# A decoder trunk step: gMLP's layer norm in two VectorE passes, other chain distances, another tile order

## The chip, the cores and the metric

The kernel runs on one core of a Trainium2 chip. A core has five engines that work side by side and wait for each other by semaphores: TensorE (PE in the profile; its weight loads are PEld) multiplies matrices, VectorE (DVE) and ScalarE (ACT) do elementwise work and can read PE's results in PSUM, GpSimd (POOL) does elementwise work in SBUF alone, SyncE (SP) here only issues transfers. The metric is the time on the device for one execution, in microseconds (us), as the median of several runs.

## The reference

One layer of a decoder, for 1024 prompt tokens and 64 sample tokens with the same weights. In short:

```python
x = layer_norm(ALPHA * x + 0.5 * swiglu(x, f1...), ln1_g, ln1_b)
z = x @ w_in + b_in
u, v, q, k, vm, o, ig, fg = split(z)
u, v = gelu(u), gelu(v)                                  # 4 gMLP heads of 128 columns
vn = layer_norm(v, gm_ln_g, gm_ln_b)                     # over a head's 128 columns
gm = u * (tril(W_s) @ vn + b_s)                          # inside chunks of 128 tokens
h_ml = sigmoid(o) * mlstm(silu(conv(q)), silu(conv(k)), vm, ig, fg)   # 4 mLSTM heads
mix = concat(head_rms(gm, gm_out_g), head_rms(h_ml, ml_out_g))
x = layer_norm(ALPHA * x + mix @ w_out, ln2_g, ln2_b)
x = layer_norm(ALPHA * x + 0.5 * swiglu(x, f2...), ln3_g, ln3_b)
```

The layer norm of the change is the one that makes `vn`: mean and variance over the 128 columns of a head, (v - mean) times 1/sqrt(var + eps), times a gain, plus a bias.

## The kernel before

The tokens stand in nine tiles: tiles 0 to 7 are 128 prompt tokens each, tile 8 is the 64 sample tokens. All matrix products are made in a split form: an operand is cut in a high and a low part (a copy on ACT, a subtraction on DVE, L237 and L238 for activations, L122 and L124 for weights), and the product is the sum of two or three products of parts.

The program goes through these stages: the first FFN (`Up`, `Down`), layer norm 1 with the transposes that follow it, the input projection with the gMLP and mLSTM work between its matmuls, the output projection with layer norm 2, the second FFN, layer norm 3.

**The input projection** runs token tile by token tile. `zunit` (L948 on) computes one tile: 24 matmuls for a prompt tile, 16 for the sample tile, whose token parts stand side by side so that one product fewer is needed; its two halves of the result are added when it is evicted (`add_psum`, L984 and L986, the second only for tile 8). Loops over all nine tiles are made for: `vm` (two times, columns of the mLSTM values), `gmlp_units(h)` (four times, u and v of a gMLP head) and the second half of `o`. Between them `heads(h)` makes q and k of an mLSTM head. The order is heads 0 and 1, units 0, heads 2, units 1, heads 3, `o`, units 2, units 3.

**Weights.** `Weights` keeps blocks of weights in six buffers; a set for one loop is four blocks, so up to two blocks of the next set can stand ready. In the last tile of a loop (`release`), a block is given back after each pair of its columns has been used, and the next block of the plan is then loaded, copied (L122) and subtracted (L124). The subtraction is on POOL for every second block of the input projection, otherwise on DVE.

**Background chains.** What isn't a large matmul is written as Python generators. `bg.tick()` lets each active chain run up to its next `yield`. `zunit` ticks after every `tick_every` matmuls and once at its end: with 6, four ticks in a prompt tile and three in the sample tile. `bg.until(...)` ticks, without matmuls between, until the chains named have ended. So the number of `yield`s in a chain is a distance, in ticks, between its steps. The order of ticks is the order in which instructions are written; the framework then sets each engine's queue by priority in that order and by its own estimate of when operands are ready, so the queues in the trace are not exactly in program order. All waits are put in by the framework.

**A gMLP chain** (`gmlp`, L1371 on) belongs to a head and three tiles: group (h, 0) is tiles 0 to 2, (h, 1) tiles 3 to 5, (h, 2) tiles 6 to 8. It is spawned when the third of its tiles has been evicted and has gone through GELU (L1448) into a buffer `ge`. Its steps: statistics on DVE (L1384, L1385); 1/sqrt by a power on POOL (`rsqrt`, L242 and L243); 4 yields; the normalisation on DVE (L1391); gain and bias on POOL (L1397), a multiply and an add over all three tiles; 8 yields; the product with the chunk's matrix (`pmix`, L1406); 2 yields; times u (L1412) and sums of squares on ACT (L1415); 2 yields; a second 1/sqrt on POOL; 4 yields; the last scaling into the mixer tile `y` on DVE (L1425; `y` is `ya` for tiles 0 to 3 and `yb` for the others). There are three `ge` buffers: a unit that opens a new group waits by `bg.until` for the chain that was spawned three groups earlier.

**mLSTM chains** (`mlstm(h)`) wait for the convolution of k, then three yields, then go through the chunks. Their last scaling is L1367.

**The output projection** goes over tiles 0 to 3, then 8, 4 to 7, in four column groups each. Ahead of it, a barrier `bg.until` waits for the mLSTM chains and for groups (3, 0) and (3, 1). `mix_xt(t)` transposes the mixer tile t (L251), splits it (L237, L238) and loads the residual; the first three are started at once, each later one three tiles ahead.

Of the kernel before, what the change touches and what calls it, by code (L numbers as in the profile page):

```python
# [29 lines left out]
KSC = float(P) ** -0.5  # L30
BIG = 1.0e30
WO_GROUPS = ((0, 1, 2, 3), (8, 4, 5, 6, 7))
WCOL = 528
YW = 1040
OU, OV, OQ, OK, OVM, OO, OG = 0, 512, 1024, 1536, 2048, 2560, 3072
# [67 lines left out]
class Weights:  # L103
# [10 lines left out]
    def _issue(self):  # L114
        nc = self.nc
        i = self.issued
        key = self.plan[i]
        n = 528 if key == ("o", 0, key[2]) else 512
        raw = self.pool.tile([P, WCOL], F32, tag="r", name=f"wr{i}", bufs=4)
        nc.sync.dma_start(raw[:, :n], self.src[i][:, :n])  # L120
        wt = self.pool.tile([P, 2, WCOL], F32R, tag="u", name=f"w{i}")
        nc.scalar.copy(wt[:, 0, :n], raw[:, :n])  # L122
        eng = nc.gpsimd if not key[0].startswith("wo") and i % 2 else nc.vector
        eng.tensor_sub(wt[:, 1, :n], raw[:, :n], wt[:, 0, :n].bitcast(F32))  # L124
        self.tiles[key] = wt
        self.issued += 1
# [57 lines left out]
def trunk_kernel(ctx: ExitStack, tc: tile.TileContext, a):  # L184
# [964 lines left out]

    for c in range(2):  # L1150
        wts = token_weights("vm", c)
        for t in range(NT):
            rows = _rows(t)

            def evict(p, t=t, rows=rows, c=c):
                ye = y[:rows, t, c * 260:(c + 1) * 260].rearrange("p (h e) -> p h e", h=2)
                add_psum(t, ye[:, :, 0:P], p[:, 0:256].rearrange("p (h e) -> p h e", h=2),
                         bc1[:rows, 512 + c * 256:512 + (c + 1) * 256].rearrange("p (h e) -> p h e", h=2))
                G.memset(ye[:, :, P:P + 1], 1.0)
                G.memset(ye[:, :, P + 1:P + 2], 0.0)  # L1160

            zunit(t, wts, 256, evict, "pv", release=t == 8)


    cvt = spare[:, 0:216].rearrange("p (b j) -> p b j", b=8)
# [47 lines left out]
    def mlstm(h):  # L1213
        while ("conv", "k", h) not in bg.finished:
            yield
        for _ in range(3):
            yield
        q, k = conv_out[("q", h)], conv_out[("k", h)]
        p1s, wts_, kws, p2s, cns = {}, {}, {}, {}, {}
# [151 lines left out]
    def gmlp(h, ts, ge, wsr, wss):  # L1371
# [12 lines left out]
            V.bn_stats(st[:rows], ge[:rows, j, 0:P])  # L1384
            V.bn_aggr(mv[:rows, j, :], st[:rows])  # L1385
        rsqrt(rs[:, 0:3], mv[:, :, 1], EPS, 3)
        for _ in range(4):
            yield
        for j, t in enumerate(ts):
            rows = _rows(t)  # L1390
            V.tensor_scalar(ge[:rows, j, 0:P], ge[:rows, j, 0:P], mv[:rows, j, 0:1], rs[:rows, j:j + 1],  # L1391
                            op0=ALU.subtract, op1=ALU.mult)
        parts = [(P, slice(0, 2)), (TS, slice(2, 3))] if tail else [(P, slice(0, 3))]
        for op, c0 in ((ALU.mult, 0), (ALU.add, 512)):
            for rows, js in parts:
                v = ge[:rows, js, 0:P]
                G.tensor_tensor(v, v, bc4[:rows, c0 + h * P:c0 + (h + 1) * P].unsqueeze(1).to_broadcast(list(v.shape)), op=op)  # L1397
        for _ in range(8):
            yield
        if tail:  # L1400
            nc.sync.dma_start(a["gvp"][:, hs], ge[:, 1, 0:P])
# [14 lines left out]
        yield  # L1416
        yield
        rsqrt(rs[:, 3:6], rs[:, 3:6], EPS, 3, scale=1.0 / P)
        for _ in range(4):
            yield  # L1420
        while ("m", h) not in bg.finished:
            yield
# [5 lines left out]
    def gmlp_units(h):  # L1428
        wts = token_weights("vu", h)
        bvu = bc3[:, h * 256:(h + 1) * 256]  # L1430
        wsr = m2.tile([P, P], F32, tag="wsr", name="wsr")
        wss = m2.tile([TS, TS], F32, tag="wss", name="wss")
        nc.sync.dma_start(wsr, a["wsT"][:, h * P:(h + 1) * P])
        nc.sync.dma_start(wss, a["wsS"][:, h * TS:(h + 1) * TS])
        G.tensor_tensor(wsr, wsr, tri, op=ALU.mult)
        G.tensor_tensor(wss, wss, tri_s, op=ALU.mult)
        for t in range(NT):
            rows = _rows(t)
            if t % 3 == 0:
                ge_no = 3 * h + t // 3  # L1440
                if ge_no >= 3:
                    bg.until(("gm",) + divmod(ge_no - 3, 3))
                ge = m2.tile([P, 3, 256], F32, tag="ge", name="ge", bufs=3)

            def evict(p, t=t, rows=rows, ge=ge):
                gt = ge[:rows, t % 3, :]
                add_psum(t, gt, p[:, 0:256], bvu[:rows])
                S.activation(gt, gt, AF.Gelu_apprx_tanh)  # L1448
                if t % 3 == 2:
                    bg.spawn(("gm", h, t // 3), gmlp(h, [t - 2, t - 1, t], ge, wsr, wss))  # L1450

            zunit(t, wts, 256, evict, "pgm", tick_every=6, release=t == 8)

    def heads(h):
        wt = [W.get(("qk", h, kp)) for kp in range(4)]
# [23 lines left out]


    wts = token_weights("o", 1)
    for t in range(NT):
        rows = _rows(t)

        def evict(p, t=t, rows=rows):
# [4 lines left out]
            bg.until(("epa", 2))  # L1490
            V.scalar_tensor_tensor(hml(rows, t, 2), og[:rows, 0:P], 1.0, hml(rows, t, 2), op0=ALU.add, op1=ALU.mult)

        zunit(t, wts, 256, evict, "po", tick_every=6, release=t == 8)
    bg.finished.add(("o", 1))
    nc.sync.dma_start(a["cv"], cvt)
    gmlp_units(2)
    gmlp_units(3)

    bg.newest_first = False
    bg.until(*[("epb", h) for h in range(H)], ("gm", 3, 0), ("gm", 3, 1), *[("m", h) for h in range(H)])  # L1500


    def mix_xt(t):
        rows = _rows(t)
        while t >= 6 and ("gm", 3, 2) not in bg.finished:
            yield
        put_xt(t, 0, transposes(t, [j * 130 for j in range(4)]))
        yield
        put_xt(t, 1, transposes(t, [520 + j * P for j in range(4)]))
        nc.sync.dma_start(y[:rows, t, 0:D], x1d[t * P:t * P + rows, :])  # L1510
        yield
# [243 lines left out]
```

## Time and profile before

| | us |
|---|---|
| median of 3 runs | 1951.69 (1951.45 to 1952.05) |
| profiled execution | 1949.92 |
| its span | 1948.1 |

The profile shows one execution. The span goes from its first to its last instruction. Busy times are sums per engine; a row of a group gives busy time and mean length of one instruction, then, behind a bar, how long the engine sat idle just ahead of such instructions and what ended that. A row of an order of time gives start, length, engine, line, operation, `output<-inputs`, the shape and a count; idle time ahead of it stands in square brackets with the instruction that ended it. Matmuls are pipelined: two that follow each other overlap in the rows, so a row's length over its count is not exactly the pace. Some matmul records can be missing.

The stages lie about so: first FFN up to 723 us, input projection from there to 1107 us, output projection to about 1230 us, second FFN to the end.

### The profile page before, as it was taken

What the parts mean: (1) busy time and instruction counts of PE and PEld (TensorE: products, weight loads), DVE (VectorE), ACT (ScalarE), POOL (GpSimd) and SP (SyncE); (2) the same over time, 40 slices, a digit from 0 to 9 for tenths busy, and PEclk for the clock granted to TensorE, in tenths of its full rate; (3) what the DMA queues carried; (4) which work ended last, traced back from release to release, by engine and by line L of the source; (5) the groups of instructions that cost most, each with busy time, mean ns of one, the idle gap of its engine ahead of it and who ended that gap; (6) DMA issues with size and microseconds to landing.
All of it is one profiled execution on the core that took longest, in us unless ns stands there. A gap on an engine that the chain in (4) does not pass through costs nothing.

```text
span 1948.1 us, 27285 instructions
## 1 busy us (share of the span) xinstructions
PE 1920.8 (99%) x10207; PEld 1628.4 (84%) x10207; DVE 1315.1 (68%) x2313; ACT 770.6 (40%) x1507; POOL 474.2 (24%) x404
## 2 busy tenths in 40 slices
PE   8999999999999999999999899999999999999997
PEld 7888888888788889988889899888888888888885
DVE  8876555656856585367876866986665665685657
ACT  5544444444222242164453333554444444422222
POOL 0222222222433031114423400012222222243302
PEclk9999999999999999999999999999999999999999
DMA  6444443336876533111211263244444333687643
GB/s 217 154 149 158 140 149 138 130 123 222 316 261 223 182 126 106 44 45 50 63 36 47 79 227 105 87 155 148 149 149 155 134 134 123 216 321 260 225 159 116
DMA packets 100892, 293.15 MB, mean 150 GB/s; under 512 B 19224, under 2 KB 26392, under 8 KB 97944
## 3 DMA queue, kind: packets, MB, share of 16 engines
q1 hardware_dynamic: 80600, 218.01, 34.1%
q10 hardware_dynamic: 20160, 73.41, 9.5%
q8 instruction: 80, 1.31, 0.3%
q14 instruction: 52, 0.43, 0.1%
HBM read 197.77 MB, written 93.60 MB: 150 GB/s over the span
## 4 chain that ended last, share of the span: by engine, by line
PE 55%; DVE 5%; POOL 1%; ACT 1%; issue 1%; DMA 0%; DVEq 0%; ACTq 0%; POOLq 0%
PE px L381 12%; PE pw L381 6%; PE pd L750 6%; PE pw L750 5%; PE pq L973 5%; PE pw L957 4%; PE pz L381 3%; PE pgm L957 3%; PE pv L957 3%; PE po L957 2%; PE psm L397 2%; PE psm L759 1%; PE tp L251 1%; DVE yb L306 1%; DVE yb L303 0%
## 5 line engine op out<-in xcount | busy, mean ns | idle before, releaser
L381 PE MATMUL px<-xo,uop 128*128 128x512 f32 x2112 | 504.5, 394 | 6.1 <-ACT uop L372 6.1
L381 PEld LDWEIGHTS px<-xo,uop 128*128 128x128 f32 x2112 | 392.9, 189 | 91.1 <-ACT uop L372 6.3
L373 DVE TENSOR_TENSOR uop<-ur,uop 128x512 fp32r<-128x512 f32 x264 | 193.4, 748 | 112.5 <-ACT uop L372 112.2
L381 PE MATMUL pw<-xo,uop 128*128 128x512 f32 x1056 | 250.0, 392 | 0.0
L381 PEld LDWEIGHTS pw<-xo,uop 128*128 128x128 f32 x1056 | 198.1, 188 | 44.3
L750 PE MATMUL pd<-wop,hop 128*128 128x512 f32 x960 | 227.7, 394 | 0.3 <-DVE rsq L242 0.2
L750 PEld LDWEIGHTS pd<-wop,hop 128*128 128x128 f32 x960 | 179.8, 188 | 42.8 <-DVE yb L721 0.6
L372 ACT CAST uop<-ur 128x512 fp32r<-128x512 f32 x264 | 158.5, 620 | 109.4 <-PE psm L397 69.1
L750 PE MATMUL pw<-wop,hop 128*128 128x512 f32 x792 | 188.5, 394 | 0.2 <-DVE yb L721 0.2
L237 ACT CAST wop<-wd 128x512 fp32r<-128x512 f32 x132 | 80.0, 620 | 248.0 <-DVE ya L721 123.9
L750 PEld LDWEIGHTS pw<-wop,hop 128*128 128x128 f32 x792 | 148.0, 188 | 35.8 <-DVE yb L721 1.0
L362 POOL TENSOR_TENSOR s<-ur,ur 128x1024 f32<-128x1024 f32 x18 | 43.8, 2432 | 512.6 <-DMA hd<-hw 260.9
L238 DVE TENSOR_TENSOR hw<-c,hw 128x512 fp32r<-128x512 f32 x120 | 96.6, 805 | 71.3 <-ACT hw L237 70.4
L381 PE MATMUL pz<-xo,uop 128*128 128x512 f32 x528 | 127.7, 397 | 0.0
L238 DVE TENSOR_TENSOR wop<-wd,wop 128x512 fp32r<-128x512 f32 x132 | 108.4, 832 | 27.2 <-ACT wop L237 26.7
L381 PEld LDWEIGHTS pz<-xo,uop 128*128 128x128 f32 x528 | 97.5, 188 | 22.3
L237 ACT CAST hw<-c 128x512 fp32r<-128x512 f32 x120 | 74.3, 619 | 75.9 <-DVE c L503 45.7
L957 PE MATMUL pgm<-w,xt 128*128 128x256 f32 x768 | 101.5, 288 | 1.1 <-DVE w L124 0.6
L397 PEld LDWEIGHTS psm<-uop,xs 128*128 128x128 f32 x704 | 95.3, 189 | 7.8 <-ACT uop L372 0.3
L957 PEld LDWEIGHTS pgm<-w,xt 128*128 128x128 f32 x768 | 94.7, 191 | 5.3 <-issue 3.4
L397 PE MATMUL psm<-uop,xs 128*128 128x256 f32 x704 | 98.0, 281 | 0.0
L957 PE MATMUL pw<-w,xt 128*128 128x256 f32 x768 | 97.4, 284 | 0.5 <-ACT xt L237 0.5
(341 smaller groups left out, 2849.8 us busy)
## 6 DMA issues: line engine op xcount, KB each, us to landing
hd<-hw ACTq DMA_DIRECT2D x140, 512.0 KB, 3.1
hop<-hd SPq DMA_DIRECT2D x132, 512.0 KB, 4.7
ur<-in_wu SPq DMA_DIRECT2D x94, 512.0 KB, 3.8
wd<-in_wd SPq DMA_DIRECT2D x22, 1024.0 KB, 7.3
wr<-in_ws SPq DMA_DIRECT2D x76, 256.0 KB, 2.9
hopx<-hd SPq DMA_DIRECT2D x8, 512.0 KB, 6.0
hsd<-sm SPq DMA_DIRECT2D x20, 192.0 KB, 1.9
hs<-hsd SPq DMA_DIRECT2D x18, 192.0 KB, 6.5
```

What stands on the lines that cost most here:

```text
L237: S.copy(hi, src)
L238: V.tensor_sub(dst[ix + (1,)], src, hi.bitcast(F32))
L251: TE.transpose(pv[:, j, :rows], y[:rows, t, c0:c0 + P], ident[:rows, :rows])
L306: V.scalar_tensor_tensor(yt, yt, mv[:rows, 2:3], b_t[:rows], op0=ALU.mult, op1=ALU.add)
L362: eng.tensor_tensor(s1, a21, a22, op=ALU.add)
L372: S.copy(op[:, 0], sj)
L373: V.tensor_sub(op[:, 1], sj, op[:, 0].bitcast(F32))
L381: TE.matmul(ps, lhsT=units[k // 2][:, wi, c0:c0 + P], rhs=self.xo[m][:, k, xi, :], start=start and k == 0 and j == 0, stop=k == 3 and j == ...
L397: TE.matmul(ps, lhsT=self.xs[:, which, k, :], rhs=units[k // 2][:, wi, (k % 2) * 256:(k % 2 + 1) * 256], start=first and k == 0 and wi == ...
L750: TE.matmul(p, lhsT=hop[:, hi, i * P:(i + 1) * P], rhs=wop[:, wi, :], start=start and pi == 0 and j == 0, stop=pi == len(pairs) - 1 and j ...
L957: TE.matmul(p[:, :n], lhsT=xl(t, k, xi), rhs=wk[:, wi, kk * n:(kk + 1) * n], start=(i == 0), stop=(i == last - 1))
L973: TE.matmul(p, lhsT=wt[k // 2][:, wi, c0:c0 + P], rhs=st["xt"][(c, k // 4)][:, k % 4, xi, :], start=(i == 0), stop=(i == 23))
```

## The change

1. Of the weight blocks, the odd ones among the first eight are subtracted on DVE instead of POOL.
2. Loops over all nine tiles, in `vm`, the second `o` and `gmlp_units`, take the order 0 to 5, 8, 6, 7. A group of the gMLP is spawned behind tiles 2, 5 and 7.
3. `mlstm` has five yields instead of three ahead of its first chunk.
4. The layer norm of `gmlp` is made in two DVE passes: (v - mean) times gain, which doesn't need the 1/sqrt and is issued right behind it; then times 1/sqrt, plus bias. POOL's two affine steps are gone. The yields are 5, 5, 2, 2, 7 in place of 4, 8, 2, 2, 4.
5. The barrier ahead of the output projection waits for group (3, 0) alone; `mix_xt(t)` waits for the group of its own tile.

```diff
+TOKS = (0, 1, 2, 3, 4, 5, 8, 6, 7)
...
-        eng = nc.gpsimd if not key[0].startswith("wo") and i % 2 else nc.vector
+        eng = nc.gpsimd if not key[0].startswith("wo") and i % 2 and i >= 8 else nc.vector
...
-        for t in range(NT):
+        for t in TOKS:
...
-            zunit(t, wts, 256, evict, "pv", release=t == 8)
+            zunit(t, wts, 256, evict, "pv", release=t == TOKS[-1])
...
-        for _ in range(3):
+        for _ in range(5):
             yield
         q, k = conv_out[("q", h)], conv_out[("k", h)]
...
         rsqrt(rs[:, 0:3], mv[:, :, 1], EPS, 3)
-        for _ in range(4):
-            yield
         for j, t in enumerate(ts):
             rows = _rows(t)
-            V.tensor_scalar(ge[:rows, j, 0:P], ge[:rows, j, 0:P], mv[:rows, j, 0:1], rs[:rows, j:j + 1],
-                            op0=ALU.subtract, op1=ALU.mult)
-        parts = [(P, slice(0, 2)), (TS, slice(2, 3))] if tail else [(P, slice(0, 3))]
-        for op, c0 in ((ALU.mult, 0), (ALU.add, 512)):
-            for rows, js in parts:
-                v = ge[:rows, js, 0:P]
-                G.tensor_tensor(v, v, bc4[:rows, c0 + h * P:c0 + (h + 1) * P].unsqueeze(1).to_broadcast(list(v.shape)), op=op)
-        for _ in range(8):
+            v = ge[:rows, j, 0:P]
+            V.scalar_tensor_tensor(v, v, mv[:rows, j, 0:1], bc4[:rows, h * P:(h + 1) * P], op0=ALU.subtract, op1=ALU.mult)
+        for _ in range(5):
+            yield
+        for j, t in enumerate(ts):
+            rows = _rows(t)
+            v = ge[:rows, j, 0:P]
+            V.scalar_tensor_tensor(v, v, rs[:rows, j:j + 1], bc4[:rows, 512 + h * P:512 + (h + 1) * P],
+                                   op0=ALU.mult, op1=ALU.add)
+        for _ in range(5):
             yield
...
         rsqrt(rs[:, 3:6], rs[:, 3:6], EPS, 3, scale=1.0 / P)
-        for _ in range(4):
+        for _ in range(7):
             yield
...
-        for t in range(NT):
+        for t in TOKS:
             rows = _rows(t)
-            if t % 3 == 0:
+            if t in (0, 3, 8):
...
-                if t % 3 == 2:
-                    bg.spawn(("gm", h, t // 3), gmlp(h, [t - 2, t - 1, t], ge, wsr, wss))
+                if t in (2, 5, 7):
+                    t0 = t // 3 * 3
+                    bg.spawn(("gm", h, t // 3), gmlp(h, [t0, t0 + 1, t0 + 2], ge, wsr, wss))
...
-    bg.until(*[("epb", h) for h in range(H)], ("gm", 3, 0), ("gm", 3, 1), *[("m", h) for h in range(H)])
+    bg.until(*[("epb", h) for h in range(H)], ("gm", 3, 0), *[("m", h) for h in range(H)])
...
-        while t >= 6 and ("gm", 3, 2) not in bg.finished:
+        while ("gm", 3, t // 3) not in bg.finished:
             yield
```

More of the change, by code (lines that the diff above doesn't have):

```diff
@@ L1448, in evict @@
                 S.activation(gt, gt, AF.Gelu_apprx_tanh)
-                if t % 3 == 2:
-                    bg.spawn(("gm", h, t // 3), gmlp(h, [t - 2, t - 1, t], ge, wsr, wss))
-            zunit(t, wts, 256, evict, "pgm", tick_every=6, release=t == 8)
+                if t in (2, 5, 7):
+                    t0 = t // 3 * 3
+                    bg.spawn(("gm", h, t // 3), gmlp(h, [t0, t0 + 1, t0 + 2], ge, wsr, wss))
+            zunit(t, wts, 256, evict, "pgm", tick_every=6, release=t == TOKS[-1])
     def heads(h):
@@ L1481, in trunk_kernel @@
     wts = token_weights("o", 1)
-    for t in range(NT):
+    for t in TOKS:
         rows = _rows(t)
@@ L1491, in evict @@
             V.scalar_tensor_tensor(hml(rows, t, 2), og[:rows, 0:P], 1.0, hml(rows, t, 2), op0=ALU.add, op1=ALU.mult)
-        zunit(t, wts, 256, evict, "po", tick_every=6, release=t == 8)
+        zunit(t, wts, 256, evict, "po", tick_every=6, release=t == TOKS[-1])
     bg.finished.add(("o", 1))
```

## The prediction

> **What bounds the kernel now.** I read the page first: the engines' shares, the slices, the chain of work that ended last.
>
> ```profile
> span 1948.1 us, 27285 instructions
> PE 1920.8 (99%) x10207; PEld 1628.4 (84%) x10207; DVE 1315.1 (68%) x2313; ACT 770.6 (40%) x1507; POOL 474.2 (24%) x404
> ...
> PE 55%; DVE 5%; POOL 1%; ACT 1%; issue 1%; DMA 0%; DVEq 0%; ACTq 0%; POOLq 0%
> ```
>
> PE is the bound: 1948.1 - 1920.8 = 27.3 us of the span are idle on it, and the change removes no matmul. So the most it can give is idle PE time, and time in which PE is busy but slow. Where that lies, the busy times by stretch tell (columns: stretch, length, then busy us and number of instructions of PE, PEld, DVE, ACT and POOL, granted clock, DMA share, GB/s):
>
> ```profile
> 0.00:20.00 20.00, 14.15 (x54) 11.01 (x55) 13.28 (x22) 14.52 (x24) 0.39 (x7) 1.00 0.90 328
> ...
> 700.00:740.00 40.00, 38.97 (x247) 34.37 (x247) 37.74 (x74) 21.10 (x38) 14.60 (x41) 1.00 0.53 171
> ...
> 850.00:900.00 50.00, 50.00 (x368) 45.62 (x367) 38.61 (x100) 32.25 (x78) 16.68 (x25) 1.00 0.11 24
> ...
> 1050.00:1100.00 50.00, 47.10 (x360) 44.30 (x359) 39.20 (x108) 13.74 (x55) 21.98 (x35) 0.97 0.11 35
> 1100.00:1130.00 30.00, 26.59 (x212) 24.56 (x211) 24.06 (x58) 14.68 (x40) 9.70 (x17) 1.00 0.47 153
> ...
> 1930.00:1948.00 18.00, 6.54 (x28) 4.67 (x26) 13.94 (x26) 2.49 (x4) 5.09 (x4) 0.77 0.29 117
> ```
>
> The first and the last stretch hold 5.9 and 11.5 us of the idle time, and the change touches neither. What it can reach is 2.9 us in 1050:1100, 3.4 us in 1100:1130 and about 1 us in 700:740. The third column from the right, the clock, is 0.97 in 1050:1100: there is more there than the idle time. Cut finer:
>
> ```profile
> 1070.00:1075.00 5.00, 5.00 (x44) 5.00 (x44) 2.55 (x11) 1.41 (x7) 1.96 (x5) 1.00 0.26 107
> 1075.00:1080.00 5.00, 2.17 (x13) 1.58 (x12) 4.49 (x10) 1.86 (x5) 2.17 (x3) 0.96 0.00 0
> 1080.00:1085.00 5.00, 4.93 (x30) 4.63 (x30) 4.17 (x12) 2.36 (x9) 2.78 (x5) 0.70 0.66 186
> 1085.00:1090.00 5.00, 5.00 (x43) 4.80 (x42) 4.37 (x12) 0.83 (x2) 2.94 (x5) 1.00 0.15 47
> ...
> 1106.00:1118.00 12.00, 8.59 (x62) 7.05 (x61) 10.89 (x26) 6.82 (x19) 4.41 (x8) 1.00 0.44 140
> 1118.00:1130.00 12.00, 12.00 (x101) 11.51 (x100) 8.47 (x22) 5.97 (x15) 1.05 (x2) 1.00 0.73 243
> ```
>
> Count matmuls: 1075:1085 ran 13 + 30 = 43 in 10 us, as many as 1085:1090 ran in 5. **Hole one** so costs 5.0 us: 2.9 us idle, about (1 - 0.96) x 5 + (1 - 0.70) x 5 = 1.7 us of lowered clock behind it, the rest short waits. 1106:1118 ran 62 where the next 12 us ran 101, so at that rate it lost 12 x (1 - 62/101) = 4.6 us: **hole two**. Both lie in gMLP's last head and the start of the output projection. PE's order of time shows what ended each gap:
>
> ```profile
> 1073.94 1.59 PE L957 MATMUL pgm<-w,xt 128*128 128x256 f32 x12
> 1077.30 0.94 PE L1406 MATMUL pmix<-ge,wsr 128*128 128x128 f32 x6 [1.76 <-POOL ge L1397]
> ...
> 1078.74 0.39 PE L957 MATMUL pgm<-w,xt 128*128 128x256 f32 x1 [0.51 <-ACT w L122]
> ...
> 1079.68 9.68 PE L957 MATMUL pgm<-w,xt 128*128 128x256 f32 x65 [0.56 <-DVE w L124]
> ...
> 1108.91 1.47 PE L957 MATMUL pw<-w,xt 128*128 128x256 f32 x6 [0.53 <-ACT xt L237]
> ...
> 1110.98 1.32 PE L251 MATMUL tp<-cc,ya 128*128 128x128 f32 x7 [0.59 <-DVE ge L1412]
> ...
> 1114.35 0.33 PE L251 MATMUL tp<-cc,ya 128*128 128x128 f32 x1 [1.46 <-DVE ya L1425]
> ...
> 1116.57 0.66 PE L251 MATMUL tp<-cc,ya 128*128 128x128 f32 x4 [0.71 <-DVE xt L238]
> ```
>
> Hole one begins with POOL's affine steps (L1397), hole two with the end of group (3,1) (L1412, L1425), which the barrier in front of the projection orders ahead of the first transposes.
>
> **The affine steps.** Why L1397 is late, and why the weights are late behind it:
>
> ```profile
> 1072.30 0.35 DVE L1391 TENSOR_SCALAR ge<-ge,gmv,grs 128x128 f32<-128x128 f32 x1 [1.27 <-POOL grs L243]
> ...
> 1072.56 0.87 DVE L1412 SCALAR_TENSOR_TENSOR ge<-pmix,pp,ge 128x128 f32<-128x128 f32 x3
> ...
> 1075.25 2.15 DVE L1425 SCALAR_TENSOR_TENSOR ya<-ge,grs,bc_bc 128x128 f32<-128x128 f32 x2 [1.32 <-POOL grs L243]
> ...
> 1077.32 0.41 DVE L984 TENSOR_TENSOR ge<-pgm,bc_bc 128x256 f32<-128x256 f32 x1
> ...
> 1071.40 0.86 POOL L243 TENSOR_TENSOR grs<-rsq,mh 128x3 f32<-128x3 f32 x1
> ...
> 1074.35 0.86 POOL L243 TENSOR_TENSOR grs<-rsq,mh 128x3 f32<-128x3 f32 x1
> ...
> 1075.17 2.08 POOL L1397 TENSOR_TENSOR ge<-ge,bc_bc 128x384 f32<-128x384 f32 x2
> ...
> L1425 DVE SCALAR_TENSOR_TENSOR ya<-ge,grs,bc_bc 128x128 f32<-128x128 f32 x16 | 12.9, 833 | 7.4 <-POOL grs L243 7.4
> ...
> L1425 DVE SCALAR_TENSOR_TENSOR yb<-ge,grs,bc_bc 64x128 f32<-64x128 f32 x4 | 1.3, 335 | 0.0
> ...
> L1391 DVE TENSOR_SCALAR ge<-ge,gmv,grs 128x128 f32<-128x128 f32 x32 | 9.9, 350 | 10.6 <-POOL grs L243 10.6
> ...
> L1397 POOL TENSOR_TENSOR ge<-ge,bc_bc 128x384 f32<-128x384 f32 x16 | 16.2, 1011 | 1.1 <-ACT sq L1359 0.5
> ```
>
> POOL first did another group's power (1074.35), then two steps of 1.0 us each. While it did, two L1425 took 2.15 us on VectorE where one takes 0.33, and ended when POOL ended; the eviction L984, the GELU and the weight's copy queued behind them. Removed: 12 groups of such steps, the only POOL work between a group's power and its pmix. Added: six passes in place of three, so 36 more of about 0.33 us; 12 us of VectorE by that length. The L1425 of ya alone are 16 x (0.83 - 0.33) = 8 us longer than the short form, and most of that stretch goes, so VectorE's total hardly grows.
>
> [...]
>
> New chain in hole one: power ends at 1072.26, three second passes 1.0, three L1412 that stood there 0.9: 1074.2, against 1077.30. PE wants it earlier, too. By yields, pmix now comes after 12 resumes instead of 14; with tile 8 before tiles 6 and 7 that is 16 + 24 + 24 = 64 matmuls behind tile 5 instead of 76, at 5.00/43 = 0.12 us each 1.4 us earlier, so 1074.1 where PE came to it at 1073.94 + 1.59 = 1075.5. That just meets. The weight waits (0.51 and 0.56) follow from the blocked VectorE queue and a short last tile: a tile of 16 matmuls frees buffers faster than they are refilled, one of 24 leaves 6 x 0.12 = 0.7 us more up to the third pair's use. I take all of hole one: **-5.0 us** (ends: 0, if pmix and weights stay late; -5.0).
>
> [...]
>
> **Chain distances, mLSTM's two yields.** 4+8+4 becomes 5+5+7: 23 resumes for 22. In the tile order 0..5, 8, 6, 7 a head's first group still ends in its last unit, so its buffer wait forces nothing. mLSTM starts two ticks, about 12 matmuls or 1.4 us, later; in 850:900 PE is full and VectorE has 11 us free, which hide it: 0 (ends: -1, +1, the size of one wait there).
>
> **Weight blocks 1, 3, 5, 7 to VectorE.**
>
> ```profile
> 721.71 3.53 DVE L306 SCALAR_TENSOR_TENSOR yb<-yb,bmv,bc_ln_b 128x1024 f32<-128x1024 f32 x2
> ...
> 731.56 1.28 DVE L306 SCALAR_TENSOR_TENSOR yb<-yb,bmv,bc_ln_b 128x1024 f32<-128x1024 f32 x1 [0.37 <-POOL bmv L243]
> ...
> 728.90 0.68 DVE L124 TENSOR_TENSOR w<-wr,w 128x512 fp32r<-128x512 f32 x1
> ...
> 722.17 1.99 POOL L124 TENSOR_TENSOR w<-wr,w 128x528 fp32r<-128x528 f32 x1
> ...
> 725.39 1.06 PE L251 MATMUL tp<-cc,yb 128*128 128x128 f32 x8 [0.94 <-DVE yb L306]
> ```
>
> Four subtractions of 0.68 join a VectorE that 700:740 shows 37.74 of 40 busy; but the two L306 beside POOL's subtraction took 3.53 us, one alone takes 1.28, so about 1 us comes back where 0.94 was waited. Ends: -0.9 and +1.4 (two blocks ahead of the transposes). I take 0.
>
> **Output projection after group (3,0) alone.** The first transposes no longer stand behind group (3,1). The waits that it ended, 0.59 + 1.46, and the 0.71 whose split stood behind L1425, go: **-2.8**. The 0.53, and half of the loss that isn't drawn as idle, stay: the six splits for three tiles and the weights' subtractions still crowd VectorE (10.89 of 12). In return tile 3 waits for (3,1) inside the projection, right ahead of its own matmuls: L1425 0.33, transpose, copy and split (0.7 or less each), some 2 us, partly covered by pmix of (3,2) and the next columns' first two weights: **+1.0** (ends 0 and +2).
>
> **Sum:** -5.0 - 2.8 + 1.0 = -6.8 us. The profiled execution took 1949.92 us, 1.8 more than its span, and lies 1.8 under the median of 1951.69; from the median: **1944.9 us**.
>
> **Rivals.**
> - *Both holes close whole*, tile 3's wait is hidden, the layer norm gains its 0.9: 5.0 + 4.6 + 0.9 = 10.5, **1941.2**. For it: the next 12 us run full with the same kinds of work. Against it: the splits and subtractions ahead of the first projection matmuls.
> - *The next wait takes the place.* pmix is on time by only 0.1 us; if weights stay late (1.1) and tile 3 waits its 2 us with nothing gained in hole two, the gain is 5.0 - 1.1 - 2.0 = 1.9: **1949.8**. For it: VectorE is 4.49 and 4.17 of 5 busy there and gets more.
> - *VectorE's queue becomes the bound* (slower). The first pass is issued with the power, 0.86 us on POOL (L243). If POOL stops a two-input pass as L1397 stopped L1425, the pass holds VectorE's queue for 0.86 us, and evictions and weights stand behind it: 12 x 0.86 = 10.3 us if PE feels all, with no gain left: up to **1962**. It decides where VectorE has less free than that per group: 1075:1085 leaves 10 - 4.49 - 4.17 = 1.3 us, 850:900 leaves 11 us, so only the stretch around the last head is near it.
> - *The change doesn't act*, as the instructions' order, which is not that of the program in the trace, cancels the new distances: **1951.7**.
>
> **Chances.** Forecast 0.55 (its own range 1943 to 1947.5), all closed 0.12, next wait 0.22, no effect 0.03, VectorE's queue 0.08. A measurement of this kernel can tell 0.2%, 3.9 us, from no change: under 1947.8 is faster. Faster 0.67, same 0.25, slower 0.08. The range runs from the first rival to a little over the second, 1941 to 1950.5, and leaves out the last two and the lowest tail.
>
> **What would show it.** Right: the clock row has no drop between 1050 and 1100; no L1397; L1425 near 0.33 us; PE without a wait over 0.6 us at pmix and at the first tp; POOL less busy by the 16.2 us of the full groups and their tails besides. Wrong: first passes of 0.8 us and more beside L243; a PE wait at tile 3's tp over 2 us; a new gap at 715 to 740 on DVE L124 or L306; a clock drop elsewhere.

## The result and the profile after

| | before, us | after, us |
|---|---|---|
| median of 6 runs each | 1951.25 (1950.55 to 1952.05) | 1940.45 (1939.85 to 1942.25) |
| profiled execution | 1949.92 | 1940.68 |
| its span | 1948.1 | 1938.9 |

The ratio after/before is 0.9948, with a 95% interval of 0.9938 to 0.9958: faster by 8 to 12 us, where 6.8 had been forecast. The median lies 0.55 us under the low end of the range, 1941, and 2.55 us under the low end of the forecast's own, 1943. The two profiled executions differ by 9.2 us, and that difference is followed here.

Most line numbers of the changed kernel are one higher than before (`pmix` is L1407, the last scaling L1426, the weights' subtraction L125). Its two passes are L1391 and L1397, both on VectorE, so its L1397 is not POOL's L1397 of before. In PE's rows `pd` is the last product of an FFN, `pv` is `vm`, `pgm` a unit of the gMLP, `tp` a transpose, and `pw` behind 1099 us the output projection.

The page of the changed kernel, its engines' busy times:

```profile
span 1938.9 us, 27255 instructions
PE 1916.7 (99%) x10207; PEld 1626.5 (84%) x10207; DVE 1315.0 (68%) x2353; ACT 773.8 (40%) x1509; POOL 451.4 (23%) x368
```

PE runs the same 10207 matmuls and is still the bound. Its idle time fell only from 27.3 to 1938.9 - 1916.7 = 22.2 us. The rest of the 9.2 us is time in which PE had been busy but slow, or in which short gaps are not drawn. VectorE has 40 more instructions (36 passes, 4 subtractions of weights) and the same total, 1315 us: what they cost came back from instructions that had been longer beside POOL's steps, the last scalings above all (the 32 of 128x128 took 24.5 us in sum before, 13.3 after). POOL's total fell by 22.8 us.

The busy times by stretch, in the columns of the prediction's table (length; PE, PEld, DVE, ACT, POOL; clock; DMA):

```profile
700.00:740.00 40.00, 40.00 (x257) 35.69 (x256) 38.33 (x79) 21.32 (x39) 10.78 (x38) 1.00 0.53 175
...
1050.00:1100.00 50.00, 49.23 (x399) 47.39 (x398) 38.67 (x125) 15.79 (x65) 15.11 (x29) 1.00 0.11 35
1100.00:1130.00 30.00, 28.14 (x234) 27.20 (x234) 21.54 (x59) 12.11 (x33) 3.16 (x6) 1.00 0.70 223
...
1106.00:1118.00 12.00, 12.00 (x101) 11.48 (x101) 8.05 (x25) 4.77 (x17) 1.05 (x2) 1.00 0.49 148
```

700:740 is full now, and the clock's 0.97 in 1050:1100 is 1.00. 1106:1118, hole two's old place, runs the 101 matmuls that the next 12 us ran before. What is left lies ahead of it. PE's order of time shows both places:

```profile
1071.11 0.83 PE L1407 MATMUL pmix<-ge,wsr 128*128 128x128 f32 x6
1071.69 1.78 PE L958 MATMUL pgm<-w,xt 128*128 128x256 f32 x13
1074.08 0.97 PE L958 MATMUL pgm<-w,xt 128*128 128x256 f32 x6 [0.60 <-DVE w L125]
1075.22 5.86 PE L958 MATMUL pgm<-w,xt 128*128 128x256 f32 x47 [0.17 <-POOL w L125]
...
1099.39 0.83 PE L1407 MATMUL pmix<-ge,wsr 128*128 128x128 f32 x6
1100.06 1.47 PE L252 MATMUL tp<-cc,ya 128*128 128x128 f32 x12
1103.38 0.99 PE L958 MATMUL pw<-w,xt 128*128 128x256 f32 x4 [1.85 <-ACT xt L238]
...
1106.40 7.37 PE L958 MATMUL pw<-w,xt 128*128 128x256 f32 x60
1113.61 0.61 PE L1407 MATMUL pmix<-ge,wsr 128*128 128x128 f32 x4
1114.14 0.43 PE L1407 MATMUL pmix<-ge,wss 64*64 64x128 f32 x2
1114.50 0.66 PE L252 MATMUL tp<-cc,ya 128*128 128x128 f32 x4
```

The six `pmix` of hole one wait for nothing, and of the 1.76 + 0.51 + 0.56 us of waits behind each other 0.60 + 0.17 are left. The first transposes (1100.06) wait for nothing; one wait, 1.85 us, remains, for ACT's copy of the transposed tiles. Tile 3's transposes (1114.50) come after 60 projection matmuls and a `pmix`, without a wait.

At PE's last matmul the gain is 9.5 us, of which 0.3 go again behind it. The 9.5 us can be laid out by when PE reaches the same matmul in both traces (its first or last matmul of a kind; my subtraction):

| PE reaches | before | after | gained so far | in this stretch |
|---|---|---|---|---|
| last `pd` of the first FFN | 722.44 | 722.32 | 0.1 | 0.1 |
| first `pv` (`vm`) | 752.85 | 751.41 | 1.4 | **1.3**, layer norm 1 |
| first `pgm` of head 3 | 1073.94 | 1071.69 | 2.2 | 0.8 |
| last `pgm` of head 3 | 1106.12 | 1099.27 | 6.9 | **4.6**, hole one |
| last `pw` of the projection | 1224.06 | 1214.54 | 9.5 | **2.7**, hole two |
| last matmul | 1936.35 | 1926.84 | 9.5 | 0 |

One of these cuts is not quite like for like. The six `pmix` of head 2's group (2,1) stand behind head 3's first matmuls before (1077.30) and ahead of them after (1071.11), where they take 1071.69 - 1071.11 = 0.58 us. With them on one side of the cut in both, hole one gave 4.0 us and the stretch before it 1.4. Below, "head 3" is the time from the first to the last `pgm` of head 3 with 18 `pmix` in it: 0.6 us are added where a trace has 12.

Three questions follow. Is hole one POOL's doing, and by which way: the chain through POOL, or POOL's hold on VectorE? What do the order, the distances and the barrier each carry? And where do the 1.3 us in layer norm 1 come from, which the sum put at 0?

### The profile page after: what moved, and what is told of

Read it like the earlier page. It is cut to its first block, busy times and chain, and to the rows that moved or that the text cites. A ratio compares the mean times of both kernels' runs of the same rounds, so it can differ in the third digit from the quotient of the medians.

```text
span 1938.9 us, 27255 instructions
## 1 busy us (share of the span) xinstructions
PE 1916.7 (99%) x10207; PEld 1626.5 (84%) x10207; DVE 1315.0 (68%) x2353; ACT 773.8 (40%) x1509; POOL 451.4 (23%) x368
```

## The experiments

The theory is the prediction's: POOL's affine steps make hole one, the barrier on group (3,1) makes hole two. The rivals: the new distances and the tile order make the gain, by their timing; or the next wait takes over. "+" and "-" are against the kernel named. The runs fall in three groups, each beside its own runs of the kernel before (medians 1950.85, 1950.76, 1950.38), so differences are given to that. By the same measure the change itself is 10.8 us under before.

**One part undone at a time.** First the chain: two passes back to one pass and POOL's two steps, with the old distances.

```diff
# against the changed kernel
-            V.scalar_tensor_tensor(v, v, mv[:rows, j, 0:1], bc4[:rows, h * P:(h + 1) * P], op0=ALU.subtract, op1=ALU.mult)
-        for _ in range(5):
+        for _ in range(4):
             yield
...
+            V.tensor_scalar(ge[:rows, j, 0:P], ge[:rows, j, 0:P], mv[:rows, j, 0:1], rs[:rows, j:j + 1],
+                            op0=ALU.subtract, op1=ALU.mult)
...
+                G.tensor_tensor(v, v, bc4[:rows, c0 + h * P:c0 + (h + 1) * P].unsqueeze(1).to_broadcast(list(v.shape)), op=op)
-        for _ in range(5):
+        for _ in range(8):
             yield
...
-        for _ in range(7):
+        for _ in range(4):
```

> The changed kernel with gMLP's chain of before (normalisation on VectorE, gain and bias on POOL, yields 4, 8, 4); the new tile order, barrier, mLSTM yields and weight engines stay. From the first to the last matmul of the last gMLP head (pgm, head 3) the kernel before took 32.2 us, the changed one 27.6. Theory (POOL's affine steps and what queues behind them made hole one): hole one returns, 31 to 32.5 us for that stretch, a clock drop in it, 1944 to 1946.5 us in all; L1425/1426 of ya near 0.8 us again. Rival (the tile order with its longer last tile closed hole one): 27.5 to 28.5 us, no clock drop, 1940 to 1942 us in all.

Measured: 1944.79 us (1944.2 to 1945.65), 6.1 under before (ratio 0.9968, 0.9957 to 0.998). PE's order of time in this kernel, then POOL's and VectorE's (L1398 is L1397 of before):

```profile
1076.55 0.94 PE L1407 MATMUL pmix<-ge,wsr 128*128 128x128 f32 x6 [1.49 <-POOL ge L1398]
1078.38 0.38 PE L958 MATMUL pgm<-w,xt 128*128 128x256 f32 x1 [0.89 <-ACT w L123]
...
1074.42 2.08 POOL L1398 TENSOR_TENSOR ge<-ge,bc_bc 128x384 f32<-128x384 f32 x2
...
1074.50 2.41 DVE L1426 SCALAR_TENSOR_TENSOR ya<-ge,grs,bc_bc 128x128 f32<-128x128 f32 x3 [0.58 <-POOL grs L244]
1076.94 0.42 DVE L985 TENSOR_TENSOR ge<-pgm,bc_bc 128x256 f32<-128x256 f32 x1
```

Hole one is back as it was: the wait for POOL, three L1426 that take 2.41 us beside POOL's 2.08, the eviction, GELU and weight behind them, and a half clock of 3.41 us from 1079.25. Head 3 takes 31.9 us, against 32.2 before and 28.2 after. The order of tiles, which this kernel keeps, has not closed the hole. The projection, though, gained 4.8 us in this kernel, not 2.7: all of hole two.

Then the distances alone, the order alone, and both.

```diff
# against the changed kernel: distances (5, 5, 7 to 4, 8, 4)
-        for _ in range(5):
+        for _ in range(4):
             yield
...
-        for _ in range(5):
+        for _ in range(8):
             yield
...
-        for _ in range(7):
+        for _ in range(4):
             yield
# against the changed kernel: order
-TOKS = (0, 1, 2, 3, 4, 5, 8, 6, 7)
+TOKS = (0, 1, 2, 3, 4, 5, 6, 7, 8)
...
-            if t in (0, 3, 8):
+            if t in (0, 3, 6):
...
-                if t in (2, 5, 7):
+                if t in (2, 5, 8):
```

> The changed kernel, two VectorE passes kept, with the yields of before, 4, 8, 4 in place of 5, 5, 7. Theory (the passes matter, the distances hardly): within 1 us of the changed kernel, 1939.5 to 1942, head 3 within 27.5 to 28.5 us. Rival (the distances carry the gain, since eight yields put pmix later and four put the last scaling too near its power): 1943 to 1946, with PE waits of over 0.5 us at pmix or at the first transposes of the projection.

> The changed kernel with tiles in order 0 to 8, the sample tile last in each loop. Theory (the order gives the weights 0.7 us more at each change of sets and little else): weight waits on PE of 0.5 to 1.5 us at the start of head 3's units, head 3 within 28 to 29.5 us, 1941 to 1943 us in all. Rival 1 (the order closed hole one): 31 us and more for head 3, 1944.5 to 1947. Rival 2 (the order does nothing): within 0.5 us of the changed kernel, 1940 to 1941.

> The changed kernel with both the order 0 to 8 and the yields 4, 8, 4 of before (two passes, barrier, weight engines, mLSTM yields as changed). If the small gains of the two runs that had one of these each add up: 1938.3 to 1939.2. If both took away the same 1.85 us wait: 1939.2 to 1940. If the old pair misses a buffer or a pmix together: 1941 to 1944.

Measured: 1939.89 (1939.45 to 1940.0), 1939.36 (1939.21 to 1939.51) and, both undone, 1942.20 (1940.74 to 1942.95); 11.0, 11.5 and 8.2 under before (ratios 0.9943, 0.994, 0.9956). The old order was expected at 1941 to 1943 us: a miss, as it came out about 1 us faster than the change. By the same starts of matmuls, the gain on before:

| distances, order | head 3 | projection |
|---|---|---|
| new, new (the change) | 4.0 | 2.7 |
| old, new | 3.6 | 3.9 |
| new, old | 3.7 | 3.9 |
| old, old | 1.4 | 3.8 |

Neither is needed while the other is there; without both, 2.6 us of hole one come back. That kernel's PE, at hole one:

```profile
1072.37 0.83 PE L1407 MATMUL pmix<-ge,wsr 128*128 128x128 f32 x6
1073.18 0.38 PE L958 MATMUL pgm<-w,xt 128*128 128x256 f32 x1
1074.54 0.98 PE L958 MATMUL pgm<-w,xt 128*128 128x256 f32 x6 [0.98 <-DVE w L125]
1076.25 8.00 PE L958 MATMUL pgm<-w,xt 128*128 128x256 f32 x53 [0.73 <-POOL w L125]
```

`pmix` is on time there, too. What comes back is the weights' wait, 0.98 + 0.73 us where the change has 0.60 + 0.17, and the half clock behind it, 3.41 us that cost 1.7. So the distances and the order do not hurry `pmix`; with either of them the weights come sooner, by a way that was not traced. The 1.7 us may in part be chance: PE was busy for 1.83 us in the window ahead of the drop, against 1.86 in one of the kernel before where none followed (last section), and of the four executions one, 1940.74 us with a mean clock of 0.998, is 1.3 us under the next, as if it had no such drop.

Both together cost 1.2 us at hole two, the 1.85 us wait. VectorE and ACT of the changed kernel ahead of it:

```profile
1100.18 1.89 DVE L125 TENSOR_TENSOR w<-wr,w 128x512 fp32r<-128x512 f32 x3
1101.99 0.42 DVE L985 TENSOR_TENSOR ge<-pgm,bc_bc 128x256 f32<-128x256 f32 x1
```

```profile
1102.44 0.42 ACT L1449 ACTIVATE ge<-ge 128x256 f32<-128x256 f32 x1 [1.04 <-DVE ge L985]
1102.76 1.54 ACT L238 CAST xt<-tp 128x512 fp32r<-128x512 f32 x3
```

Three weight subtractions hold the last tile's eviction, the eviction holds its GELU, and the copies of the transposes stand behind the GELU on ACT. The kernel with the old order has the same three subtractions (1.88 us from 1099.69), but ACT takes the copies ahead of the last GELU there:

```profile
1100.42 1.56 ACT L238 CAST xt<-tp 128x512 fp32r<-128x512 f32 x3
1102.06 0.42 ACT L1449 ACTIVATE ge<-ge 64x256 f32<-64x256 f32 x1
```

The next run is to get the eviction of the changed kernel forward by giving the odd weight blocks of the projection's first set to POOL:

```diff
# against the changed kernel
-        eng = nc.gpsimd if not key[0].startswith("wo") and i % 2 and i >= 8 else nc.vector
+        pool = i % 2 and i >= 8 if not key[0].startswith("wo") else key[:2] == ("wo0", 0) and i % 2
+        eng = nc.gpsimd if pool else nc.vector
```

> The changed kernel with two of the first four output weight blocks subtracted on POOL, which is idle from 1096.8 to 1104.2 us there. Theory (what is left of hole two, 1.85 us, is ACT's copy of the transposes behind a GELU behind VectorE's three subtractions of weights): the wait shrinks to under 1 us, 1939 to 1940 in all. Rival (POOL's 1.3 us per block makes the last weights late instead): 1940.5 to 1942, a PE wait at pw ended by POOL w.

A miss: 1940.86 us (1940.75 to 1942.47), 9.5 under before, and the wait is 2.0 us instead of 1.9. VectorE and POOL:

```profile
1100.02 2.37 DVE L126 TENSOR_TENSOR w<-wr,w 128x512 fp32r<-128x512 f32 x2
1102.31 0.41 DVE L986 TENSOR_TENSOR ge<-pgm,bc_bc 128x256 f32<-128x256 f32 x1
...
1100.28 1.56 POOL L126 TENSOR_TENSOR w<-wr,w 128x512 fp32r<-128x512 f32 x1 [3.63 <-ACT w L123]
```

Two subtractions beside POOL's one take 2.37 us, longer than three in the changed kernel, where POOL is idle (1.89).

Next the barrier, back to groups (3,0) and (3,1):

```diff
# against the changed kernel
-    bg.until(*[("epb", h) for h in range(H)], ("gm", 3, 0), *[("m", h) for h in range(H)])
+    bg.until(*[("epb", h) for h in range(H)], ("gm", 3, 0), ("gm", 3, 1), *[("m", h) for h in range(H)])
...
-        while ("gm", 3, t // 3) not in bg.finished:
+        while t >= 6 and ("gm", 3, 2) not in bg.finished:
```

> The changed kernel with the barrier on groups (3,0) and (3,1) ahead of the projection, transposes waiting as before. From the last matmul of head 3 to the last of the projection the kernel before took 117.9 us, the changed one 115.3. Theory (the barrier put group (3,1) ahead of the first transposes): 117 to 118.5 us for that stretch, PE waits at tp ended by L1426 or L1413, 1942 to 1943.5 us in all. Rival (hole two closed because group (3,1) is no longer held by POOL and ends sooner anyway): 115 to 116 us, 1940 to 1941.5.

Measured: 1946.08 us (1945.23 to 1946.94), 4.8 under before (ratio 0.9975, 0.9965 to 0.9984). The mechanism is there and larger than expected. PE, VectorE and POOL:

```profile
1099.13 0.83 PE L1407 MATMUL pmix<-ge,wsr 128*128 128x128 f32 x6
1105.33 0.76 PE L1407 MATMUL pmix<-ge,wsr 128*128 128x128 f32 x2 [5.37 <-DVE ge L1397]
...
1104.84 0.87 DVE L1397 SCALAR_TENSOR_TENSOR ge<-ge,grs,bc_bc 128x128 f32<-128x128 f32 x3 [0.26 <-POOL grs L244]
...
1103.65 0.21 POOL L243 TENSOR_SCALAR rsq<-gmv 128x3 f32<-128x3 f32 x1 [7.07 <-DVE gmv L1386]
```

With the new chain, group (3,1) has 7 ticks at its end. The barrier runs them off without matmuls between, and the same ticks carry group (3,2) up to its `pmix`. The projection's transposes stand behind a `pmix` of (3,2) in PE's queue, whose layer norm has only begun: 5.37 us of nothing, and 6.83 us of half clock (1103.55 to 1110.38).

**Parts alone, on the kernel before.** The new chain (two passes, 5, 5, 7) by itself, and the chain with the new barrier. The edits are the change's own (points 4 and 5), with the old order.

> The kernel before with the new gMLP chain alone (two VectorE passes, yields 5, 5, 7); old order, barrier, weight engines, mLSTM yields. Theory (the passes close hole one, the old barrier with the new, late distances makes hole two worse, as in the run with the old barrier): head 3 within 27.5 to 29 us, a PE wait of 3 to 6 us at pmix ahead of the projection, a clock drop behind it, 1946 to 1949.5 us in all. Rival 1 (the new chain alone brings nearly all): 1941 to 1944. Rival 2 (without the order hole one stays): head 3 over 31 us, 1949 to 1953.

> The kernel before with two parts of the change alone: the new gMLP chain (two passes, yields 5, 5, 7) and the new barrier; old order, old weight engines, three mLSTM yields. Theory (these two carry all but layer norm 1's 1.4 us): 1939.4 of the run with the old order plus 1.4, so 1940.3 to 1941.3. Rival (the order and the yields prepare the barrier's gain): 1942.5 and more.

Measured: the chain alone 1947.83 us (1947.15 to 1949.87), 2.9 under before (0.9986, 0.9976 to 0.9995); with the barrier 1940.83 (1940.47 to 1941.63), 9.6 under (0.9951, 0.9934 to 0.9967). The waits of PE with the chain alone (total, times, longest):

```profile
PE pmix L1406 <- DVE ge L1396: 5.2, 1, 5.2
PE tp L251 <- DVE yb L306: 1.6, 2, 0.9
```

Head 3 takes 28.5 us, so hole one is closed, but for 0.3 us, without order, weights or barrier; and the old barrier takes 2.8 us back, as above. The two parts together carry nearly all of the change, and the layer norm's 0.9 us waits stay in both.

**The weights, and mLSTM's yields.**

```diff
# against the changed kernel: weights
-        eng = nc.gpsimd if not key[0].startswith("wo") and i % 2 and i >= 8 else nc.vector
+        eng = nc.gpsimd if not key[0].startswith("wo") and i % 2 else nc.vector
# against the changed kernel: mlstm
-        for _ in range(5):
+        for _ in range(3):
```

> The changed kernel with weight blocks 1, 3, 5, 7 subtracted on POOL again. From the last matmul of the first FFN (pd) to the first of vm (pv) the kernel before took 30.4 us, the changed one 29.1; the prediction had 0 for this. Theory (POOL's subtraction stretched layer norm 1's two passes beside it): 30.2 to 30.8 us for that stretch, a PE wait of 0.7 to 1.2 us at tp ended by the layer norm's pass, 1941 to 1942.5 us in all. Rival (the gain there comes from the tile order or from chance in the order of instructions): 29 to 29.5 us, 1940 to 1941.

> The changed kernel with three yields ahead of mLSTM's chunks, as before. Theory (the two yields do nothing that can be measured): within 0.7 us of the changed kernel, 1939.7 to 1941.2, and 897 to 1072 us of the span as in it. Rival (they keep the chunks clear of gMLP's first group and bring the 1 us that the changed kernel gains between 897 and 1072 us): 1941 to 1942.5, the gain there gone.

Measured: 1942.05 us (1941.02 to 1942.58) with the old weights, 8.7 under before; 1940.63 (1940.36 to 1942.82) with three yields, 10.1 under. In the first trace PE falls back by 1.3 us against the changed kernel between the last `pd` and the first `pv`, and stays 1.4 us behind from there to the end. In the second it is 0.6 us ahead at the last `pd`, up to 1.0 us behind between 850 and 1000 us, and 0.2 to 0.5 us ahead from 1040 us to the end: the yields move work there, and nothing of it is left at the end. VectorE of the kernel with the old weights, then of the changed one:

```profile
721.71 3.53 DVE L307 SCALAR_TENSOR_TENSOR yb<-yb,bmv,bc_ln_b 128x1024 f32<-128x1024 f32 x2
```

```profile
721.59 2.47 DVE L307 SCALAR_TENSOR_TENSOR yb<-yb,bmv,bc_ln_b 128x1024 f32<-128x1024 f32 x2
```

**Which way POOL hurts.** Elementwise work on POOL that nothing waits for: three additions of 128x256 in each group, behind the first power. If POOL's steps cost by the chain that leads through them, this costs nothing; if by POOL's hold on VectorE, it costs what the affine steps cost. First with operands that are always there, then with the power's result as an input, so that they run where the affine steps ran.

```diff
# against the changed kernel, first form
+        for _ in range(3):
+            G.tensor_tensor(spare[:, 216:472], bc4[:, 0:256], bc4[:, 256:512], op=ALU.add)
# second form
+        for _ in range(3):
+            G.tensor_tensor(spare[:, 216:472], bc4[:, 0:256], rs[:, 0:1].to_broadcast([P, 256]), op=ALU.mult)
```

> The changed kernel with three additions of 128x256 on POOL behind each group's first power, about 2.2 us as the affine steps took, into scratch that no other step reads; nothing waits for them but POOL's own queue. It tells POOL's hold on VectorE apart from the chain's length. Theory A (POOL's steps hold VectorE's two-input passes while they run): passes L1391, L1397 and L1426 stretched, means of 0.5 us and more for 128x128 where the changed kernel shows 0.35 to 0.47, some loss on PE, 1941 to 1944. Theory B (only the chain through POOL mattered): means within 0.05 us of the changed kernel's, 1940 to 1941.

> The changed kernel with three POOL products of 128x256 behind each group's first power into scratch that nothing reads, now with the power's result as one input, so that they run where the affine steps ran. Theory A (POOL's two-input steps hold VectorE's passes): the second pass, L1397 in the changed kernel, and the last scaling L1426 stretched from means of 0.35 to 0.47 us to 0.55 us and more; PE waits of 1 to 4 us somewhere between 860 and 1110 us; 1941 to 1945. Theory B (the hold matters only where a long row of POOL steps meets a chain, as it did in the gates): means up by less than 0.1 us, 1940 to 1941.5.

The first form took 1947.35 us (1945.18 to 1949.26), 3.4 under before, and met neither expectation: the steps had no input to wait for, and the framework set them some 100 to 300 us earlier in POOL's queue, beside the mLSTM gates' chain in `vm`. VectorE's and POOL's order there, then the same gate step of the changed kernel:

```profile
757.10 0.78 DVE L1057 TENSOR_TENSOR gtmp<-gtmp 128x36 f32<-128x36 f32 x1
...
758.74 0.20 DVE L1061 TENSOR_TENSOR gtmp<-gtmp 128x36 f32<-128x36 f32 x1
758.97 0.62 DVE L1062 TENSOR_SCALAR gtmp<-gtmp 128x36 f32<-128x36 f32 x1
...
747.02 19.38 POOL L1393 TENSOR_TENSOR spare<-bc_bc 128x256 f32<-128x256 f32 x22
```

```profile
756.33 0.18 DVE L1062 TENSOR_SCALAR gtmp<-gtmp 128x36 f32<-128x36 f32 x1
```

Small steps of the gates' chain went from 0.18 to 0.62 us, PE waited 3.5 us for that chain's end, and two stretches of half clock followed; PE went from 0.6 us ahead of the changed kernel to 5.4 behind there. Another 1.3 us went at the output projection, with a third such stretch (the mean clock of this trace is 0.996, of the changed kernel's 0.998). It says little of gMLP's chain.

The second form ran in place and took 1948.22 us (1947.23 to 1949.35), 2.2 under before (0.9987, 0.9978 to 0.9997): of the change's gain some 8 us are gone, with a chain that does not take its values from the added work. That, too, met neither expectation: the loss is larger than either had, the second pass is up by 0.09 us on the mean, and the last scaling of `ya` not at all. The added work is 23.8 us of POOL, where the three forms of the affine steps had 16.2 + 5.9 + 3.8 = 25.9 in the trace of before. VectorE's groups in this kernel, then in the changed one (busy, mean ns; L1399 and L1428 are its second pass and last scaling):

```profile
L1391 DVE SCALAR_TENSOR_TENSOR ge<-ge,gmv,bc_bc 128x128 f32<-128x128 f32 x32 | 15.0, 471 | 0.7
L1399 DVE SCALAR_TENSOR_TENSOR ge<-ge,grs,bc_bc 128x128 f32<-128x128 f32 x32 | 13.4, 443 | 8.3 <-POOL grs L244 7.9 <-POOL grs L1380 0.3
L1428 DVE SCALAR_TENSOR_TENSOR ya<-ge,grs,bc_bc 128x128 f32<-128x128 f32 x16 | 6.7, 443 | 2.2 <-POOL grs L244 2.2
```

```profile
L1391 DVE SCALAR_TENSOR_TENSOR ge<-ge,gmv,bc_bc 128x128 f32<-128x128 f32 x32 | 13.2, 415 | 0.7
L1397 DVE SCALAR_TENSOR_TENSOR ge<-ge,grs,bc_bc 128x128 f32<-128x128 f32 x32 | 10.6, 354 | 8.5 <-POOL grs L244 8.4
L1426 DVE SCALAR_TENSOR_TENSOR ya<-ge,grs,bc_bc 128x128 f32<-128x128 f32 x16 | 7.1, 466 | 1.0 <-POOL grs L244 1.0
```

The passes wait for the power no longer than before (8.3 and 8.5 us), so POOL's own queue is not what holds them; it holds the last scaling of `ya` by 1.2 us more in sum. The means hide two kinds of pass: 9 of the 32 second passes took 0.44 to 0.81 us beside an added step, the others 0.34 to 0.35. The loss is spread: 2.6 us up to head 3, 1.4 in it, 4.0 between its last matmul and the settled projection, the last with a PE wait of 3.8 us for ACT's `xt` and a half clock of 3.41 us. So it is not hole one that comes back, which the old chain cost 3.8 us, but more in all, at other places. How the longer passes lead to the 3.8 us wait was not traced, and instructions that are added can change the queues' order, as the first form shows.

## Why the prediction was right in kind and short in size

| step of the prediction | forecast | measured | by |
|---|---|---|---|
| hole one | -5.0 | -4.0 | starts of matmuls, like for like; the old chain alone brings 3.8 back |
| order and distances make `pmix` "just meet" | part of it | not `pmix`; either keeps the weights on time | both undone |
| hole two | -2.8 | -3.9 | three of the four order/distance kernels |
| tile 3's wait | +1.0 | 0 | PE at 1114.50 |
| not foreseen: copies behind the last GELU | 0 | +1.2 | new order and new distances together |
| weight blocks | 0 | -1.4 | old weights alone |
| mLSTM's yields | 0 | 0 | three yields |
| 752 to 1074 | 0 | -1.4 | starts of matmuls, like for like; 1.0 of it in both kernels with parts alone |

- **Right: the two holes and their makers.** Undoing the chain opens hole one again, undoing the barrier opens hole two. The half clock is gone, L1397's work on POOL is gone, and the sum over VectorE did not grow. The -5.0 counts 1.7 us of lowered clock as gone with the hole: no run shows a rule for that, but the clock in 1050:1100 went from 0.97 to 1.00, and with the old chain a half clock of 3.41 us stood behind the hole again. The sign "L1425 near 0.33" came for 29 of 32: three of the changed kernel's L1426, at 0.70, 1.28 and 1.36 us, stand beside other work of POOL, and the two longest make the mean of 0.466 for `ya`.
- **Wrong: the weight blocks at 0.** The prediction had the right row, two L306 at 3.53 us beside POOL's subtraction, and named 0.9 as the end of the gain. It then set four subtractions on VectorE against it. They cost next to nothing: VectorE went only from 37.74 to 38.33 of 40 us, as the pair came down from 3.53 to 2.47 us. The term was mis-sized; it measured 1.4. Of that, 1.0 is PE's drawn idle time in 700:740 (38.97 busy, then 40.00); the rest was not traced.
- **Wrong: +1.0 for tile 3.** I counted a wait "right ahead of its own matmuls". 60 projection matmuls, 7.37 us, lie between; group (3,1)'s last scaling ended at 1110.81 and its transposes come at 1114.50. The cover was 3.7 us longer than the need.
- **Right by cancelling: -1.8 for hole two with tile 3.** Its trace shows -2.7, but as 3.9 gained and 1.2 given back by a wait that the prediction did not name. It had expected the first wait of this kind, 0.53 us for ACT's `xt`, to stay, for "six splits and the weights' subtractions". The subtractions are one half of the cause; the other is the last GELU ahead of the copies on ACT, as the kernel with the old order has the subtractions without the wait.
- **The margin of 0.1 us at `pmix`** on which the second rival hung was not the limit. With the old order and distances `pmix` is still on time.
- **The barrier is worth more with the new chain than the prediction could see.** It was costed against the old distances. The chain alone makes the barrier's wait 5.2 us, and the new barrier is then worth 6.7 us (the projection takes 120.8 us with the chain alone, 114.0 with the barrier added). With the old chain the projection gained 4.8 us, in a kernel that has the new order and weights as well; the barrier alone on the old chain was not run.
- **Slower rival: no.** POOL's power held no pass: 15 of the changed kernel's passes and scalings of 128x128 lay wholly beside one of its powers (128x3 or 128x8, 0.85 us and more each) and took 0.343 to 0.354 us, and those beside no work of POOL 0.332 to 0.355. The first passes' mean of 0.415 us is made by two of 32: 2.02 us beside a POOL product of 128x1040, 0.98 beside a subtraction of weights; the others took 0.31 to 0.36. Beside wide POOL work they were held: with the old chain three L1426 took 2.41 us beside 2.08 us of affine steps.
- **How POOL's steps cost** is settled in part. Signs of both ways are there: with the old chain `pmix` waits for POOL, and POOL's added work alone cost some 8 us in all, where the old chain cost 4.7 in the same kernel (6.1 under before for 10.8). Which share of hole one's 4.0 us each has is open, as the added work lost its time at other places.

The first rival, "both holes close whole" at 1941.2, is near the measured time, but by luck: neither hole closed whole (4.0 of 5.0 and 2.7 of 4.6), the layer norm gave 1.3 where it had 0.9, and 1.4 came from a stretch that it did not name.

The fastest kernel run is the change with the old tile order: 1939.36 us (1939.21 to 1939.51), ratio 0.994 (0.9925 to 0.9955). All four of its runs lie under the changed kernel's fastest, 1939.85; their intervals against before overlap, so a lead of about 1 us is likely and not settled.

## What to carry to other kernels

In this kernel VectorE makes the evictions and weights that PE waits on, and 23.8 us of elementwise work on POOL that nothing waits for cost some 8 us: in such a kernel, look for VectorE rows that end with a POOL row, and at single rows, as a mean of 32 can be made by two of them. A barrier is costed with the chain that it drains: a chain with other distances makes another wait of it, so test the two together. Parts of a change can stand in for each other: undo them singly and in pairs before one is called needed or useless.

## What the runs showed of the hardware

**POOL's and VectorE's steps were longer beside each other.** Beside one POOL subtraction of 128x512 VectorE's weight subtractions took 2.37 us for two, against 1.89 for three alone. All six of the changed kernel's passes and scalings of 128x128 over 0.4 us, and all 20 such last scalings of the kernel before, end 0.145 to 0.154 us behind the end of a POOL step, of 64x128 or wider; none stands beside a power of 128x3 or 128x8 alone. POOL's steps vary, too: in the kernel with the bound POOL load three added ones took 2.00 us at one place and 2.82 at another, where one of them took 1.43 us beside three L1428 that kept their 0.34. Even a TENSOR_SCALAR of 128x36 with one input went from 0.18 to 0.62 us while the TENSOR_TENSOR of that size beside it mostly stayed at 0.20. That is not shown to be a matter of the form: L1057, a TENSOR_TENSOR of that size, took 0.78 us there, and a pair of such steps starts every 0.88 us (758.74, then 759.62), as POOL's additions do (19.38 / 22 = 0.88).

**The drops of the clock lie on a grid.** In the trace of before the clock's record begins at 11.22 us, and the clock goes to 0.50 at 1079.60 and at 1939.75, 313 and 565 times 3.4133 us later; the first drop lasts 3.41 us, the second goes on to the end. In that of the changed kernel it goes to 0.50 once, at 1932.09, 563 times 3.4133 us behind 10.39. Of this grid's windows at full clock, those with less than 2.5 us of PE time had 1.32, 0.41 and 0.00 us of it where a drop came next, and 1.86, 2.08, 2.29 and 1.96 where none did. The busy times in such windows, first of the kernel with old order and distances (a drop followed), then of before at hole two (none followed), then of the changed kernel in a stretch off its grid and in the window on it:

```profile
1072.71:1076.12 3.41, 1.83 (x12) 1.26 (x10) 3.31 (x10) 2.62 (x6) 1.20 (x1) 1.00 0.16 26
1076.12:1079.53 3.41, 3.28 (x15) 3.28 (x16) 3.38 (x11) 1.14 (x8) 1.25 (x3) 0.50 0.76 223
```

```profile
1110.32:1113.73 3.41, 1.86 (x13) 1.35 (x12) 2.36 (x9) 1.68 (x7) 2.38 (x5) 1.00 0.56 180
```

```profile
1099.99:1103.40 3.41, 1.56 (x16) 1.32 (x14) 3.41 (x10) 2.37 (x6) 0.00 (x0) 1.00 0.42 119
1099.24:1102.65 3.41, 2.29 (x21) 2.05 (x19) 3.21 (x8) 2.37 (x6) 0.00 (x0) 1.00 0.21 54
```

With 1.83 of 3.41 us busy the clock fell, with 1.86 it did not. That is no sharp edge: moving a window by 0.02 us moves its busy time by as much, and behind PE's last work in the kernel with the bound POOL load, 1.80 us busy in 1933.36:1936.77, it fell only one window later. The changed kernel's last gap leaves 1.56 in a window that begins at 1099.99, but its grid cuts the gap in two, with 2.29 and more in each, and no drop came. A drop like the first of before, 3.41 us at 0.50, costs 1.7 us where PE is busy. The changed kernel's times could hold one in some executions alone: four lie between 1939.85 and 1940.68 with a mean clock of 0.998, two at 1941.88 and 1942.25 with 0.997; no trace of the latter two was taken, so this stays a reading.
